# Down pass of a mixture of experts: one half of the features in 64 rows of a bank, the last pair's halves in two banks, the one-hot rows ahead of the down condition

## The chip, the cores and the metric

The kernel runs on one core of one Trainium2 chip. The metric is the device time of one execution in microseconds (us). Three executions of the kernel before took 1164.79, 1169.04 and 1176.58 us; the median is 1169.04 us. TensorE is the matrix engine, VectorE (DVE), ScalarE (ACT) and GpSimd (POOL) do the work on vectors, SyncE (SP) issues DMAs. PSUM is the accumulator memory that TensorE writes, 8 banks of 128 rows x 512 numbers.

## The reference

Two decoder layers over 256 tokens of 1024 features. Each has a token-mixing sublayer (retention, pooling and a gated delta rule, not touched here) and a mixture of experts; each ends in a layer norm of a weighted input plus the sublayer's output. The part that matters is the mixture: a coarse top-1 over 4 groups, then a top-2 over the 4 experts of that group.

```python
combine = jnp.einsum('nk,nke->ne', weights, jax.nn.one_hot(expert_id, N_EXPERTS, dtype=f32))
out = jnp.zeros((B * T, D), f32)
for e in range(N_EXPERTS):
    hdn = jax.nn.silu(xt @ w_gate[e]) * (xt @ w_up[e])
    out = out + combine[:, e:e + 1] * (hdn @ w_down[e])
...
x = layer_norm(DEEPNORM_ALPHA * x + ffn_out, ln2_g[l], ln2_b[l], dtype)
```

## The kernel before

**Slots.** The 16 experts are worked off in 8 pairs, and two pairs make a quad q (pairs 2q and 2q+1; `second` is true for the latter). Each expert of a quad has 32 slots for tokens. A one-hot matrix (`quad_slots`, L875, made by GpSimd from quad 1 on) gathers the tokens of a quad into 128 columns (`gather`, L888).

**One pair.** `gate_up` (L1026) computes gate and up projections of both experts, four column tiles of TensorE at a time (32 columns each), into a bank `gus`; ScalarE and VectorE make silu(gate) x up (L1029, L1030). `turned` (L1035, L1037) transposes the result into `hT`. `down` (L1044) multiplies by the down weights: 4 contraction steps k, four column tiles j, 16 matmuls into `bank_t`. In before, tile j holds expert `j // 2` of the pair and half `j % 2` of the 1024 features, so a half of the features lies in two pieces of 32 rows. `store` (L1052) copies the four pieces to the rows of `y` that belong to the pair.

**One quad.** When both pairs of a quad are stored, the 128 rows of `y` are the quad's outputs by slot. `slot_rows` (L1057 to L1062) transposes the one-hot matrix into `gT2` and finds each slot's weight `wqs`, through the bank `bank_c`; `weighed` (L979, L980) scales `y` by it and splits it into a rounded part `hi` and a rest `lo`; `scatter` (L1074) adds it to the tokens' rows in the accumulators `acc` with eight matmuls. `gather` also goes through `bank_c`.

**Order.** The program is written in Python and scheduled; `tc.issue_after(x)` holds what follows back until x is issued, and instructions on one engine run in the order that results. `tc.If` is a branch on a register, taken by TensorE, VectorE and ScalarE apart, and loaded from a table of kinds for each pair (`load`, L1083). Experts with more than 32 tokens take the branch `overflow` (L990), which does a whole expert for up to 128 tokens and adds it to `acc` (L1019). The two branches of a pair stand between `gate_up` and `turned`. Weights come through a ring of 1 MB pieces (`fetch`), issued by SyncE when TensorE has freed a piece.

**The end of a layer.** After the last pair's `down` the first half of the quad (`front`, rows 0 to 63, pair 6) is scattered by eight matmuls (L1155), GpSimd zeroes those rows of `gT2` (L1156), and the last pair's output is weighed straight from `bank_t` in four pieces of 32 rows (L1160, on ScalarE L979 and on VectorE L980) and scattered (L1164). The layer norm follows: `bn_stats` (L246) over four halves, and the rest of its chain.

Of the kernel before, what the change touches and what calls it, by code (L numbers as in the profile page):

```python
# [15 lines left out]
ALU = mybir.AluOpType  # L16
AX = mybir.AxisListType
# [12 lines left out]
NE = 16  # L30
# [69 lines left out]
def trunk(ctx: ExitStack, tc: tile.TileContext, x, w_in, pool_w, pool_scale, conv_w, A_log, dt_bias, gdn_norm_w,  # L100
          w_branch, w_out, ln1_g, ln1_b, rc_w, rc_b, rf_w, rf_b, w_gate, w_up, w_down, ln2_g, ln2_b, consts, out,
          dbg=None):
    nc = tc.nc
# [202 lines left out]
    tbs = [slice(0, P), slice(P, T)]  # L306

    for l in range(DEPTH):
# [4 lines left out]
        done = None  # L313
        for b in range(2):
            done = transpose_rows(xt[:, b, :], b, split_evac(xh, xl), done)
# [54 lines left out]
        for i in range(2):  # L370
            for xp, src in enumerate((xh, xl)):
                for j in range(4):
                    k = 4 * i + j
# [371 lines left out]
        done = None  # L745
# [232 lines left out]
        def weigh(h, r, src, w):  # L978
            nc.scalar.activation(h, src, AF.Identity, scale=w)  # L979
            nc.vector.scalar_tensor_tensor(r, src, w, h, op0=ALU.mult, op1=ALU.subtract)  # L980
# [56 lines left out]
            nc.vector.tensor_copy(hT, p)  # L1037
            return hT, done

        def down(pair, hT):  # L1040
            for k in range(4):
                for j in range(4):
                    e = 2 * pair + j // 2
                    done = nc.tensor.matmul(bank_t[32 * j:32 * j + 32, :], hT[:, k, 32 * (j // 2):32 * (j // 2) + 32],  # L1044
                                            units[e][4 + k // 2][k % 2][:, sides[j % 2]], start=k == 0, stop=k == 3,
                                            tile_position=(0, 32 * j))
            return done

        def store(pair):
            for j in range(4):  # L1050
                at = 64 * (pair % 2) + 32 * (j // 2)
                nc.scalar.copy(y[at:at + 32, sides[j % 2]], bank_t[32 * j:32 * j + 32, :])  # L1052

        def slot_rows(G, q):
            p = bank_c
            for b in range(2):
                nc.tensor.transpose(p[:, tbs[b]], G[b], ident)  # L1057
            for b in range(2):
                nc.tensor.matmul(p[:, T:T + 4], G[b], comb[:, b, 4 * q:4 * q + 4], start=b == 0, stop=b == 1)  # L1059
            nc.scalar.copy(gT2[:, q % 2], p[:, 0:T])  # L1060
            nc.vector.tensor_tensor(w4, p[:, T:T + 4], C("quad"), op=ALU.mult)  # L1061
            nc.vector.tensor_reduce(wqs[q % 2], w4, axis=AX.X, op=ALU.add)  # L1062

        def weighed(q):
            for half in range(2):
                s = slice(half * 512, half * 512 + 512)
                weigh(hi[:, s], lo[:, s], y[:, s], wqs[q % 2])

        def scatter(q):
            for half in range(2):  # L1070
                s = slice(half * 512, half * 512 + 512)
                for yy in (hi, lo):
                    for b in range(2):
                        nc.tensor.matmul(acc[b][half], gT2[:, q % 2, tbs[b]], yy[:, s], start=False, stop=False)  # L1074

        wqs, w4 = (small("mx", [P, 1]), small("pg", [P, 1])), small("ce", [P, 4])
        fetch(held)
# [31 lines left out]
        for pair in range(NE // 2):  # L1109
            q, second = divmod(pair, 2)  # L1110
            own, other = gus[pair % 2], gus[(pair + 1) % 2]
            last_pair = pair == NE // 2 - 1
            some = (kinds[0] | kinds[1]) & 1
            with tc.If(some > 0):
                gate_up(pair)
            if q < 3:
                for i in range(2):
                    done = gather(xgs[(q + 1) % 2], Gs[q + 1], [4 * second + 2 * i, 4 * second + 2 * i + 1], i,
                                  bank_c[:, 256 * i:256 * i + 256])
            for i in range(2):  # L1120
                e = 2 * pair + i
                with tc.If(kinds[i] > 1):
                    overflow(e, units[e], own, other)
                if e + 1 < NE:
                    picked = picks(nc.gpsimd, e + 1)
            fetch(12 * pair + 8 + held)
            if q and not second:
                weighed(q - 1)
            with tc.issue_after(done.ins):
                hT, done = turned(pair)  # L1130
            with tc.issue_after(done.ins):
                if second:
                    slot_rows(Gs[q], q)
                elif q:
                    scatter(q - 1)
            if last_pair:
                break
            with tc.If(some > 0):
                down(pair, hT)
                store(pair)  # L1140
            fetch(12 * pair + 12 + held)
            with tc.issue_after(done.ins):
                kinds = load(plan[0:1, 2 * pair + 2:2 * pair + 4])
            if second and q < 2:
                with tc.issue_after(picked.ins):
                    Gs[q + 2] = quad_slots(q + 2)
        front, last = slice(0, 64), slice(64, 128)
        downed = down(NE // 2 - 1, hT)
        for s in sides:
            weigh(hi[front, s], lo[front, s], y[front, s], wqs[1][front])  # L1150
        with tc.issue_after(downed.ins):
# [3 lines left out]
                        nc.tensor.matmul(acc[b][half], gT2[front, 1, tbs[b]], yy[front, s], start=False, stop=False)  # L1155
        nc.gpsimd.memset(gT2[front, 1].bitcast(F32), 0.0)  # L1156
        for half, s in enumerate(sides):
            for i in range(2):
                r, at = slice(64 + 32 * i, 96 + 32 * i), 64 * i + 32 * half
                weigh(hi[r, s], lo[r, s], bank_t[at:at + 32, :], wqs[1][r])  # L1160
        for b in range(2):
            for half, s in enumerate(sides):
                for yy in (hi, lo):
# [41 lines left out]
```

## Time and profile before

| | |
|---|---|
| median of three runs | 1169.04 us |
| profiled execution, its own time | 1180.57 us |
| its span, first to last instruction | 1178.8 us |
| mean granted TensorE clock | 0.944 of full speed |
| expert stage of layer 0, of layer 1 | about 324 to 590 us, about 910 to 1170 us |

Times in a timeline are microseconds from the start of the span. A row gives start, duration, engine, line and operation; the bracket is the idle time of that engine ahead of the row and what ended it. PE is TensorE, PEld its weight loads, a `q` behind a name the engine's sequencer, which loads registers and branches. The granted clock of 1.00 is 2.4 GHz, 0.50 is 1.2 GHz.

### The profile page before, as it was taken

How to read it: one execution, taken by the hardware profiler on the slowest of the kernel's cores; microseconds unless marked ns; L12 is line 12 of the kernel's file. 1: busy time of each engine (PE TensorE's matmuls, PEld its weight loads, DVE VectorE, ACT ScalarE, POOL GpSimd, SP SyncE). 2: the span in 40 equal slices, each digit the busy share in tenths (PEclk: the TensorE clock that was granted, in tenths of full speed). 3: DMA queues.
4: the chain of work that ended last, by engine and by line, in shares of the span. 5: the costliest groups of instructions: out<-in, count | busy, mean ns of one | idle time of the engine just before them, and what ended most of it. 6: DMA issues, size and time to landing. Idle time of an engine off the chain costs nothing. (4 is left out here: it accounts for less than half of the span.)

```text
span 1178.8 us, 15440 instructions
## 1 busy us (share of the span) xinstructions
PE 1061.1 (90%) x5595; PEld 705.6 (60%) x5595; DVE 470.0 (40%) x962; ACT 394.9 (33%) x618; POOL 174.8 (15%) x226
## 2 busy tenths in 40 slices
PE   7999989999789798899979999999997789799995
PEld 6778678877444354544457777788774444354442
DVE  5786356557401110111267773565565001001014
ACT  4774354453210211111147552544542111202111
POOL 2030030210401101000010400202103110100011
PEclk9999989999889898999979999999999979899996
DMA  9634457657478998849265253675665693947931
GB/s 328 210 117 142 161 196 250 196 197 259 175 273 315 393 391 304 326 144 391 82 233 178 83 179 108 232 253 193 215 221 209 240 394 128 394 153 267 357 108 37
DMA packets 112789, 266.20 MB, mean 226 GB/s; under 512 B 4760, under 2 KB 5184, under 8 KB 112672
## 3 DMA queue, kind: packets, MB, share of 16 engines
q1 hardware_dynamic: 111136, 261.14, 62.0%
q0 software_dynamic: 1248, 3.01, 1.0%
q8 instruction: 69, 1.13, 0.4%
q10 hardware_dynamic: 288, 0.52, 0.1%
q14 instruction: 48, 0.39, 0.1%
HBM read 290.88 MB, written 1.05 MB: 248 GB/s over the span
## 5 line engine op out<-in xcount | busy, mean ns | idle before, releaser
L292 DVE TENSOR_TENSOR W<-R,W 128x1024 fp32r<-128x1024 f32 x148 | 184.2, 1247 | 111.7 <-PE a L298 88.0
L291 ACT CAST W<-R 128x1024 fp32r<-128x1024 f32 x150 | 157.5, 1053 | 168.5 <-PE a L297 148.8
L296 PE MATMUL a<-W,X 128*128 128x512 f32 x504 | 202.4, 403 | 3.0 <-ACT W L291 2.8
L297 PE MATMUL a<-W,X 128*128 128x512 f32 x504 | 200.4, 399 | 0.0
L298 PE MATMUL a<-W,X 128*128 128x512 f32 x496 | 194.1, 398 | 4.1 <-DVE W L292 4.0
L984 POOL TENSOR_SCALAR s_wsm<-cst,s_pos 128x128 f32<-128x128 f32 x64 | 45.9, 727 | 450.0 <-PE t L1003 243.5
L296 PEld LDWEIGHTS a<-W,X 128*128 128x128 f32 x504 | 95.9, 190 | 25.9 <-ACT W L291 4.3
L298 PEld LDWEIGHTS a<-W,X 128*128 128x128 f32 x496 | 93.7, 189 | 26.7 <-DVE W L292 7.8
L297 PEld LDWEIGHTS a<-W,X 128*128 128x128 f32 x504 | 95.6, 190 | 20.8 <-issue 2.3
L1052 ACT COPY yh<-t 32x512 f32<-32x512 f32 x56 | 32.3, 577 | 113.7 <-PE t L1044 113.2
L888 PE MATMUL t<-t,xt 128*128 128x128 f32 x240 | 40.0, 323 | 19.1 <-DVE s_ce L1061 12.8
L888 PEld LDWEIGHTS t<-t,xt 128*128 128x128 f32 x240 | 35.5, 227 | 29.1 <-issue 19.8
L1026 PE MATMUL g<-M,X 128*32 128x512 f32 x256 | 42.4, 686 | 9.3 <-DVEq L1099 9.3
L1044 PE MATMUL t<-M,zs 128*32 128x512 f32 x256 | 49.1, 757 | 1.3 <-DVE zs L1037 1.3
L1026 PE MATMUL t<-M,X 128*32 128x512 f32 x288 | 42.7, 593 | 0.0
L998 DVE TENSOR_TENSOR ul<-ul,t 128x256 f32<-128x256 f32 x14 | 5.3, 417 | 91.8 <-PE t L995 91.8
L1044 PE MATMUL t<-R,zs 128*32 128x512 f32 x160 | 39.5, 800 | 0.7 <-issue 0.7
L1030 DVE TENSOR_TENSOR ul<-ul,t 64x512 f32<-64x512 f32 x8 | 5.5, 692 | 83.1 <-ACT ul L1029 55.9
L1026 PE MATMUL g<-R,X 128*32 128x512 f32 x160 | 37.8, 626 | 0.0
L298 PE MATMUL a<-W,yh 128*128 128x512 f32 x96 | 37.4, 389 | 0.0
L296 PE MATMUL a<-W,yh 128*128 128x512 f32 x96 | 37.3, 389 | 0.0
L297 PE MATMUL a<-W,yl 128*128 128x512 f32 x96 | 37.3, 389 | 0.0
(534 smaller groups left out, 1688.7 us busy)
## 6 DMA issues: line engine op xcount, KB each, us to landing
R<-in_w_in_dram SPq DMA_DIRECT2D x55, 1024.0 KB
M<-in_w_gate_dram SPq DMA_DIRECT2D x34, 1024.0 KB
M<-in_w_up_dram SPq DMA_DIRECT2D x34, 1024.0 KB
M<-in_w_down_dram SPq DMA_DIRECT2D x32, 1024.0 KB
R<-in_w_down_dram SPq DMA_DIRECT2D x20, 1024.0 KB
R<-in_w_gate_dram SPq DMA_DIRECT2D x18, 1024.0 KB
R<-in_w_branch_dram SPq DMA_DIRECT2D x12, 1024.0 KB
R<-in_w_up_dram SPq DMA_DIRECT2D x12, 1024.0 KB
```

The lines of the kernel that those rows point to most:

```text
L291: nc.scalar.copy(h, src)
L292: nc.vector.tensor_sub(lo, src, h)
L296: nc.tensor.matmul(acc, hi, wh, start=first, stop=False)
L297: nc.tensor.matmul(acc, lo, wh, start=False, stop=False)
L298: nc.tensor.matmul(acc, hi, wl, start=False, stop=last)
L888: done = nc.tensor.matmul(view[:, i, :], xks[b][:, k, :], picks[b], start=b == 0, stop=b == 1)
L984: last = eng.tensor_scalar(gg[:, b, :], iota, start, pos[:, b, e:e + 1], op0=ALU.add, op1=ALU.is_equal)
L998: nc.vector.tensor_mul(hoT[:, s], hoT[:, s], bank_c[:, s])
L1026: nc.tensor.matmul(p[32 * j:32 * j + 32, :], xgs[e // 4 % 2][:, k, e % 4 * SLOTS:(e % 4 + 1) * SLOTS], units[e][j // 2 + 2 * (k // 4)][k % ...
L1030: nc.vector.tensor_mul(hh[64:128, :], hh[64:128, :], p[64:128, :])
L1044: done = nc.tensor.matmul(bank_t[32 * j:32 * j + 32, :], hT[:, k, 32 * (j // 2):32 * (j // 2) + 32], units[e][4 + k // 2][k % 2][:, sides[ ...
L1052: nc.scalar.copy(y[at:at + 32, sides[j % 2]], bank_t[32 * j:32 * j + 32, :])
```

## The change

Four edits. (1) `down` gives tile j half `j // 2` and expert `j % 2`, so that one half of the features fills 64 neighbouring rows, and `store` is two copies of 64 x 512 in place of four of 32 x 512. (2) For the last pair the two halves go to two banks, `bank_t` and `bank_c`, and it is weighed in two pieces of 64 rows in place of four. (3) The condition around `down` is held back until `ready`, the last instruction of `slot_rows` or `scatter` of that pair. (4) In the last quad `weighed(2)`, `scatter(2)` and `slot_rows(3)` are written ahead of the overflow branches of pairs 6 and 7.

```diff
-        def down(pair, hT):
+        def down(pair, hT, banks):
             for k in range(4):
                 for j in range(4):
-                    e = 2 * pair + j // 2
-                    done = nc.tensor.matmul(bank_t[32 * j:32 * j + 32, :], hT[:, k, 32 * (j // 2):32 * (j // 2) + 32],
-                                            units[e][4 + k // 2][k % 2][:, sides[j % 2]], start=k == 0, stop=k == 3,
+                    e = 2 * pair + j % 2
+                    done = nc.tensor.matmul(banks[j // 2][32 * j:32 * j + 32, :], hT[:, k, 32 * (j % 2):32 * (j % 2) + 32],
+                                            units[e][4 + k // 2][k % 2][:, sides[j // 2]], start=k == 0, stop=k == 3,
                                             tile_position=(0, 32 * j))
         def store(pair):
-            for j in range(4):
-                at = 64 * (pair % 2) + 32 * (j // 2)
-                nc.scalar.copy(y[at:at + 32, sides[j % 2]], bank_t[32 * j:32 * j + 32, :])
+            r = slice(64 * (pair % 2), 64 * (pair % 2) + 64)
+            for half, s in enumerate(sides):
+                nc.scalar.copy(y[r, s], bank_t[64 * half:64 * half + 64, :])
...
+            def quarter():
+                if second:
+                    return slot_rows(Gs[q], q)
+                if q:
+                    return scatter(q - 1)
+                return done
+
+            if q == 3:
+                if not second:
+                    weighed(q - 1)
+                ready = quarter()
             for i in range(2):
                 e = 2 * pair + i
                 with tc.If(kinds[i] > 1):
...
-            if q and not second:
+            if 0 < q < 3 and not second:
                 weighed(q - 1)
             with tc.issue_after(done.ins):
                 hT, done = turned(pair)
-            with tc.issue_after(done.ins):
-                if second:
-                    slot_rows(Gs[q], q)
-                elif q:
-                    scatter(q - 1)
+            if q < 3:
+                with tc.issue_after(done.ins):
+                    ready = quarter()
             if last_pair:
                 break
-            with tc.If(some > 0):
-                down(pair, hT)
+            with tc.issue_after(ready.ins), tc.If(some > 0):
+                down(pair, hT, [bank_t] * 2)
                 store(pair)
...
-        downed = down(NE // 2 - 1, hT)
+        ends = (bank_t, bank_c)
+        downed = down(NE // 2 - 1, hT, ends)
...
         for half, s in enumerate(sides):
-            for i in range(2):
-                r, at = slice(64 + 32 * i, 96 + 32 * i), 64 * i + 32 * half
-                weigh(hi[r, s], lo[r, s], bank_t[at:at + 32, :], wqs[1][r])
+            weigh(hi[last, s], lo[last, s], ends[half][64 * half:64 * half + 64, :], wqs[1][last])
```

How the program's order moves, at the three places of which the prediction speaks. In the rows, `t`, `g` and `a` are banks of PSUM, `mix` and `yl` are `hi` and `lo`, `yh` is `y`, `zs` is `hT`, `t_240` is `gT2`, `M` and `R` are weights. A bracket names what the instruction waits for.

TensorE, pair 1 of layer 0, from `slot_rows` to the first matmul of `down`, before:

```order
L1057 MATMUL t_2297<-cst,t_239_2229 128x128 x2
L1059 MATMUL t_2297<-s_comb_2282,t_239_2229 128x4 x2
L1138 REGISTER_ALU x2
L1138 COMPARE_AND_BRANCH
L1044 MATMUL t_2296<-M_6_82,zs_2299 32x512 [waits DMAHW1_49,DMAHW4_49,DVE_49,Activation_49]
```

The same place in the change:

```order
L1057 MATMUL t_2297<-cst,t_239_2229 128x128 x2
L1059 MATMUL t_2297<-s_comb_2282,t_239_2229 128x4 x2
L888 MATMUL t_2297<-t_239_2229,xt 128x128 [waits DVE_49,Pool_49]
L1148 REGISTER_ALU x2
L1148 COMPARE_AND_BRANCH
L1044 MATMUL t_2296<-M_6_82,zs_2299 32x512 [waits DMAHW4_49,DMAHW1_49]
```

One of the eight matmuls that gather for the next quad (L888), which waits for VectorE and GpSimd, has come to stand between `slot_rows` and the condition; the other seven stay behind `down`. Pair 3 and both pairs of layer 1 read the same.

ScalarE, the same pair, before:

```order
L1138 REGISTER_ALU x2
L1138 COMPARE_AND_BRANCH
L1052 COPY yh_2291<-t_2296 32x512 [waits DVE_49,PE_49,Pool_49]
L1052 COPY yh_2291<-t_2296 32x512 x3
L1138 UNCONDITIONAL_BRANCH
L1138 UNCONDITIONAL_BRANCH [waits Activation_49]
L1060 CAST t_240_2230<-t_2297 128x256 [waits DVE_49,PE_49]
L892 COPY X_219_2149<-t_2297 128x256 [waits DVE_49,PE_49]
```

In the change:

```order
L1060 CAST t_240_2230<-t_2297 128x256 [waits DVE_49,PE_49]
L1148 REGISTER_ALU x2
L1148 COMPARE_AND_BRANCH
L1052 COPY yh_2291<-t_2296 64x512 [waits PE_49,Pool_49]
L1052 COPY yh_2291<-t_2296 64x512
L1148 UNCONDITIONAL_BRANCH
L1148 UNCONDITIONAL_BRANCH [waits Activation_49]
L892 COPY X_219_2149<-t_2297 128x256 [waits DVE_49,PE_49]
```

The cast that frees `bank_c` (L1060) has moved from behind the condition and its four copies to ahead of it, and the copies are two; VectorE's two small instructions on `bank_c` (L1061, L1062) have moved in the same way.

TensorE, end of pair 5 into `gate_up` of pair 6, layer 0, before:

```order
L1138 UNCONDITIONAL_BRANCH
L1138 UNCONDITIONAL_BRANCH [waits PE_49]
L1083 TENSOR_LOAD s_rmv_2247
L1114 REGISTER_ALU x2
L1114 COMPARE_AND_BRANCH
L1026 MATMUL g_2298<-R_1_72,X_219_2149 32x512 [waits DMAHW2_49,DMAHW0_49,Activation_49]
```

In the change:

```order
L1148 UNCONDITIONAL_BRANCH [waits PE_49]
L1074 MATMUL a_2131<-mix_273_2327,t_240_2230 128x512 [waits Activation_49]
L1074 MATMUL a_2133<-mix_273_2327,t_240_2230 128x512
L1074 MATMUL a_2132<-mix_273_2327,t_240_2230 128x512 [waits Activation_49]
L1074 MATMUL a_2131<-yl_2328,t_240_2230 128x512 [waits DVE_49]
L1074 MATMUL a_2133<-yl_2328,t_240_2230 128x512
L1074 MATMUL a_2134<-mix_273_2327,t_240_2230 128x512
L1074 MATMUL a_2132<-yl_2328,t_240_2230 128x512 [waits DVE_49]
L1074 MATMUL a_2134<-yl_2328,t_240_2230 128x512
L1084 TENSOR_LOAD s_rmv_2247
L1115 REGISTER_ALU x2
L1115 COMPARE_AND_BRANCH
```

All eight matmuls of `scatter(2)` now stand between `down` of pair 5 and the load of pair 6's kinds; before, three stood ahead of `down` of pair 6 and five behind it. `weighed(2)` has moved with them, behind the store of pair 5 on ScalarE. In pair 6, `slot_rows(3)` now stands behind `down`, where before it stood between `turned` and `down` of pair 7.

## Rows read from the trace of the kernel before

**Rows 1.** The page, busy time and share of the span of each engine.

```profile
PE 1061.1 (90%) x5595; PEld 705.6 (60%) x5595; DVE 470.0 (40%) x962; ACT 394.9 (33%) x618; POOL 174.8 (15%) x226
```

**Rows 2.** Waits of TensorE, expert stages of layers 0, 1 (total, times, longest).

```profile
PE t L888 <- DVE s_ce L1061: 6.3, 2, 3.2
...
PE t L888 <- DVE s_ce L1061: 6.5, 2, 3.2
```

**Rows 3.** Timeline, layer 0, pair 1 into pair 2 (start, us, engine, line, idle).

```profile
380.84 0.51 PE L1059 MATMUL t<-s_comb,t 128*128 128x4 f32 x4
...
381.27 3.74 PE L1044 MATMUL t<-M,zs 128*32 128x512 f32 x32
381.56 2.70 POOL L875 TENSOR_SCALAR t<-cst,s_rst 128x32 f32<-128x32 f32 x8
...
385.09 2.34 ACT L1052 COPY yh<-t 32x512 f32<-32x512 f32 x4 [6.77 <-PE t L1044]
...
388.17 1.83 PE L888 MATMUL t<-t,xt 128*128 128x128 f32 x8 [3.16 <-DVE s_ce L1061]
390.04 0.37 ACT L892 COPY X<-t 128x256 f32<-128x256 f32 x1 [2.21 <-PE t L888]
...
390.46 1.79 PE L888 MATMUL t<-t,xt 128*128 128x128 f32 x8 [0.46 <-ACT X L892]
```

**Rows 4.** Stretches, layer 0: us, busy by engine, granted clock, DMA share, GB/s.

```profile
534.40:536.40 2.00, 0.07 (x2) 0.07 (x2) 0.69 (x1) 0.65 (x2) 1.70 (x3) 1.00 1.04 391
...
538.60:543.90 5.30, 5.30 (x33) 1.88 (x32) 0.18 (x1) 0.00 (x0) 0.00 (x0) 0.68 1.04 384
...
463.30:466.70 3.40, 3.40 (x20) 0.78 (x22) 0.42 (x1) 0.00 (x0) 0.00 (x0) 0.50 1.05 388
```

**Rows 5.** Timeline, layer 0, pair 5 into pair 7.

```profile
527.28 0.59 PE L1026 MATMUL g<-R,X 128*32 128x512 f32 x1
...
527.65 2.34 ACT L1052 COPY yh<-t 32x512 f32<-32x512 f32 x4 [6.76 <-PE t L1044]
...
536.34 1.34 ACT L979 ACTIVATE mix<-yh,s_mx 128x512 fp32r<-128x512 f32 x2 [1.22 <-DVEq L1122]
...
536.91 0.42 DVE L1037 COPY zs<-g 128x256 f32<-128x256 f32 x1 [1.07 <-PE g L1035]
...
537.37 1.42 DVE L980 SCALAR_TENSOR_TENSOR yl<-yh,s_mx,mix 128x512 fp32r<-128x512 f32 x2
...
538.62 5.35 PE L1044 MATMUL t<-M,zs 128*32 128x512 f32 x32
...
545.26 4.05 PE L1026 MATMUL t<-M,X 128*32 128x512 f32 x33
```

**Rows 6.** Timeline, layer 0, the last pair's tail.

```profile
586.11 0.49 PE L1155 MATMUL a<-mix,t 64*128 64x512 f32 x1
586.22 0.68 ACT L979 ACTIVATE mix<-t,s_pg 32x512 fp32r<-32x512 f32 x1 [1.47 <-PE t L1044]
...
587.70 0.68 ACT L979 ACTIVATE mix<-t,s_pg 32x512 fp32r<-32x512 f32 x1 [0.81 <-DVE yl L980]
...
588.70 0.73 PE L1164 MATMUL a<-mix,t 128*128 128x512 f32 x2 [0.48 <-POOL t L1156]
...
589.76 1.29 DVE L246 BATCH_NORM_STATS2 s_lnst<-a 128x6 f32<-128x512 f32 x2 [0.59 <-PE a L1164]
590.01 1.04 ACT L291 CAST W<-R 128x1024 fp32r<-128x1024 f32 x1 [1.63 <-DMA R<-in_w_in_dram]
...
594.99 1.30 DVE L246 BATCH_NORM_STATS2 s_lnst<-a 128x6 f32<-128x512 f32 x2 [0.95 <-PE a L1164]
```

**Rows 7.** One line, L1083: register loads on TensorE's sequencer (ns min/median/max).

```profile
L1083 PEldq TENSOR_LOAD <-s_rmv x16: 538/545/557, 317.9 to 1139.9; - x16
```

**Rows 8.** Timeline, layer 1, the last pair's tail.

```profile
1163.26 0.73 PE L1164 MATMUL a<-mix,t 128*128 128x512 f32 x2 [0.48 <-POOL t L1156]
...
1168.28 1.29 DVE L246 BATCH_NORM_STATS2 s_lnst<-a 128x6 f32<-128x512 f32 x2 [0.93 <-PE a L1164]
```

More of the change, by code (lines that the diff above doesn't have):

```diff
@@ L1061, in slot_rows @@
             nc.vector.tensor_tensor(w4, p[:, T:T + 4], C("quad"), op=ALU.mult)
-            nc.vector.tensor_reduce(wqs[q % 2], w4, axis=AX.X, op=ALU.add)
+            return nc.vector.tensor_reduce(wqs[q % 2], w4, axis=AX.X, op=ALU.add)
         def weighed(q):
@@ L1073, in scatter @@
                     for b in range(2):
-                        nc.tensor.matmul(acc[b][half], gT2[:, q % 2, tbs[b]], yy[:, s], start=False, stop=False)
+                        done = nc.tensor.matmul(acc[b][half], gT2[:, q % 2, tbs[b]], yy[:, s], start=False, stop=False)
+            return done
         wqs, w4 = (small("mx", [P, 1]), small("pg", [P, 1])), small("ce", [P, 4])
@@ L1119, in trunk @@
                                   bank_c[:, 256 * i:256 * i + 256])
+            def quarter():
[3 more added lines that the diff above has]
+                    return scatter(q - 1)
+                return done
+            if q == 3:
+                if not second:
+                    weighed(q - 1)
+                ready = quarter()
             for i in range(2):
```

## The prediction

> **What bounds the kernel now.** I read the page first: TensorE is busy 90% of the span [rows 1], so time is won where it stands still or runs at half clock. Next the waits of TensorE in the two expert stages: no transfer of any size is on the list, and beside the branches the largest wait that the change touches is the gather L888 waiting for the small VectorE instruction L1061, twice in each layer, 3.2 us each time [rows 2]. The timelines show the three places where the change acts. I call them A, B and C.
>
> A is the way from pair 1 to pair 2 and from pair 3 to pair 4: four places. `down` ends at 381.27 + 3.74 = 385.01; TensorE then stands for 3.16 us, because ScalarE makes four copies (2.34 us) before the cast L1060 and VectorE's L1061, which free the bank that the gather needs. A second wait of 0.46 us follows, for ScalarE's copy L892 [rows 3]. After such waits the clock is down: once the stretch behind it ran at 0.50 for 3.4 us [rows 4].
>
> B is the way from pair 5 over pair 6 to pair 7, once in a layer. There `gate_up` of pair 6 begins at 527.28, before ScalarE even starts to copy the result of `down` at 527.65: no gap at all [rows 5].
>
> C is the tail of a layer. The last pair's four weighings take turns on ScalarE and VectorE, since all read one bank: ScalarE's second piece starts only at 587.70, released by VectorE, though its first ended at 586.90. In layer 0 the third piece stands moreover behind a cast of the next layer's weights, which waits for a transfer until 590.01 [rows 6].
>
> The sum is made against the profiled execution, 1180.57 us; it is 11.5 us slower than the median of the three runs (1169.04), so I carry the difference over to the median.
>
> **A: the gather's wait, four places.** Cast and VectorE's pair now run as soon as `slot_rows` ends (380.84 + 0.51 = 381.35), so the 3.16 us behind `down` go. In exchange one gather matmul stands ahead of `down`, with `down` queued behind it. It needs four of GpSimd's eight one-hot instructions L875, which begin at 381.56 and take 2.70 us: half is 1.35, so 382.91. I allow 0.3 for the matmul and the branch behind it: `down` starts at 383.2 in place of 381.27 and ends at 383.2 + 3.74 = 386.9. Then seven gather matmuls; the fifth still waits for L892, now behind two copies in place of four. Rows do not make a ScalarE instruction longer: 128 rows take 1.34 / 2 = 0.67 us [rows 5], 32 rows 0.68 [rows 6]. So two copies take half of 2.34, 1.17, plus 0.37: 386.9 + 0.1 + 1.17 + 0.37 = 388.5. The last gathers take 1.79: 390.3, in place of 390.46 + 1.79 = 392.25 [rows 3]. That is 1.95 per place, say 2.0. No row has a wait ahead of `down`, so bounds: if it drops the clock there, `down` loses 3.4 us of time at half speed, 1.7, and 0.3 is left; if no clock is lost, the 1.7 of the stretch at 0.50 come on top, 3.7 [rows 4]. I take 2.0, the middle, because waits of this length are seen with the fall and without. Sum of A: -8.0 (-1.2 to -14.8).
>
> **B: scatter(2) moves ahead of pair 6, twice.** Added: TensorE waits for the chain behind `down` of pair 5. From 527.65 two copies, 1.17; ScalarE's first L979, 0.67, to 529.5, its second to 530.2; VectorE's two L980, 1.42 / 2 = 0.71 each, end at 530.9 [rows 5]. The last two matmuls wait for that, and behind them TensorE's sequencer has yet to load pair 6's kinds, 0.55 [rows 7], and to branch: 531.7. Queued behind it is `gate_up` of pair 6, which everything of that pair waits for. Price: 531.7 - 527.3 = 4.4. Removed: `down` of pair 6 need not wait for the scatter. `hT` is ready at 536.91 + 0.42 = 537.33, `down` began at 538.62: 1.2 saved after 0.1 for the signal. Behind it the five matmuls went until 545.26, after `down` ended at 538.62 + 5.35 = 543.97: 1.3 [rows 5]. In their stead come four small ones of `slot_rows(3)`, about 0.9 with the turn of bank, by 0.51 for the second half of them [rows 3]: 0.4 saved. In pair 7 they hid behind VectorE's copy of `hT`; I count nothing for their going. B is 4.4 - 1.2 - 0.4 = 2.8 per layer.
>
> Then the clock: the stretch from 534.40 stood nearly idle for 2 us, and of the 5.3 us from 538.60 the mean clock is 0.68 [rows 4]. 0.32 of 5.3 is 1.7 us lost. B's new wait is like it, so I add 1.7 with a chance of 0.7, 1.2. Sum of B: +8.0 for two layers (+5.6 to +9.0).
>
> The Trainium skill (TensorEngine Tiling (Array Packing), Key Properties) says that a change of tiling mode drains TensorE. `scatter(2)` between `down` and `gate_up` makes two such changes where there was none; the trace agrees in so far as `gate_up` began within the last wave of `down`. By the rule four changes would cost some 0.3 us each, an estimate from that overlap, and the sum would end at 1163; by the rows they lie inside gaps already counted, and it ends at 1162.
>
> **C: the tail, twice.** The work up to L1155 stays. The two halves lie in two banks, so ScalarE does them back to back: 586.22 + 0.68 + 0.68 = 587.6; VectorE, 0.71 each, ends at 588.4. L1164 starts at 588.70 as before, held by GpSimd's memset, and now all eight matmuls follow at once. The four `bn_stats` run from about 589.6 for 1.29 + 1.30, to 592.2; before, the last two ended at 594.99 + 1.30 = 596.29 [rows 6]. Layer 0: -4.1. The next layer's first weights were there at 590.01, ahead of its new beginning. Layer 1: from 1163.26 the first `bn_stats` comes about 0.9 later, 1164.2, and the four end at 1166.8, in place of 1168.28 + 1.29 = 1169.57 [rows 8]: -2.8. Sum of C: -6.9 (-2.8, if layer 0 hides it, to -7.5).
>
> **Costed at nothing.** In pairs 2 and 4 the five scatter matmuls move from behind `down` to ahead of it; the same matmuls stand on the path, and the shorter store makes up for the later `down`. Bounds: with all four copies kept there, ScalarE would be 1.17 late [rows 5], and a gain is left out because no wait goes. The new order of column tiles changes no count: `gate_up` already alternates the two experts from tile to tile, 33 records in 4.05 us [rows 5], `down` has 32 in 3.74 [rows 3]; the difference, 0.2 per pair either way, is the bound, and I take 0 because both include other work's gaps. SyncE issues the same transfers in the same order.
>
> **The sum.** -8.0 + 8.0 - 6.9 = -6.9: 1173.7 for the profiled execution, 1162 at the median, -0.6%.
>
> **The rivals.** (1) A gives nothing: the hoisted gather's wait drops the clock in `down`. For it: the wait stands behind small transposes. Against: it is half as long as the one it replaces. -1.2 + 8.0 - 6.9 = -0.1, so 1169. (2) A gives everything and B keeps its clock: -14.8 + 5.6 - 6.9 = -16.1, so 1153. For it: TensorE has eight matmuls inside B's wait; against: they are spread over 4 us. (3) Slower: B's wait drops the clock for all of `gate_up` of pair 6, from 527.28 to 534.40 [rows 4, 5], 7.1 us more. B is then 2 x (2.8 + 7.1) = 19.8, the total +4.9: 1174. It decides once B is over 14.9, a loss of clock of 4.7 us in each layer. Against: no stretch of rows 4 lost more than 1.7. The Trainium skill (TensorE: Matmul & The Clock Gate, Part 1: The HAM clock gate) makes low clock the resting state, released by activity alone; by that, a wait with few matmuls in it costs the work behind it, as in (3), and rows 4 agree. (4) Layer 0's tail hides its gain behind the next layer's weights: -2.8, 1166. Against: [rows 6], 590.01.
>
> **How the numbers follow.** Forecast 0.45 (1158 to 1166), (1) 0.20, (2) 0.22, (3) 0.08, (4) 0.05. 1% of 1169 is about 12 us, about what a measurement of this kernel can tell from no change. Faster by more than that needs a time under 1157: most of (2), 0.20. Slower by it needs over 1181, beyond (3): 0.05. Within: 0.75. The range leaves out the far end of (2) and (3): 1152 to 1171.
>
> **What would show it.** A: the wait of L888 for L1061 is gone; a new one of 1 to 2 us ahead of `down` in pairs 1 and 3, released by GpSimd. B: L1074 waits for ScalarE and VectorE behind pair 5, and `gate_up` of pair 6 begins 4 to 5 us after `down`. C: two L979 and two L980 on the last bank rows, overlapping, and `bn_stats` in one run. I am wrong if the gather ahead of `down` waits for all eight of GpSimd's instructions, if B's gap is over 6 us, or if layer 1's first matmul does not come earlier against the end of pair 7.

## The result: 1161.4 us, 1.0% faster

| | before | the change |
|---|---|---|
| median of 16 runs each | 1175.08 us | 1161.37 us |
| lowest and highest | 1164.79, 1179.44 us | 1156.88, 1167.58 us |
| ratio, 95% interval | | 0.990 (0.987 to 0.993) |
| profiled execution, its own time | 1180.57 us | 1162.66 us |
| its span, mean granted clock | 1178.8 us, 0.944 | 1160.9 us, 0.962 |

The ratio stands for 11.7 us less (8.7 to 14.8). With more runs the median of the kernel before rose by 6 us, from the 1169.04 that the prediction started from. So the gain was 5 us larger than the 6.9 of the sum, and that the time itself lies beside the predicted 1162 is luck: the two differences cancel.

The page of the change, busy time and share of the span of each engine; [rows 1] are those of before:

```profile
PE 1045.4 (90%) x5595; PEld 703.6 (61%) x5595; DVE 466.9 (40%) x958; ACT 376.1 (32%) x586; POOL 174.9 (15%) x226
```

ScalarE has 32 instructions less, 28 copies and 4 weighings. TensorE has as many as before and is busy 15.7 us less; its mean granted clock is 0.962 in place of 0.944.

Waits of TensorE in the expert stage of layer 0, after (waiting line, releaser, total us, times, longest), then of layer 1:

```profile
PE t L888 <- POOL t L875: 3.3, 2, 1.6
PE a L1074 <- ACT mix L979: 2.7, 3, 2.1
...
PE a L1074 <- ACT mix L979: 2.9, 3, 2.1
PE t L888 <- POOL t L875: 2.2, 2, 1.1
```

The wait of the gather for L1061 [rows 2] is gone. In its place the gather ahead of `down` waits for GpSimd, twice in a layer, and the scatter behind pair 5 waits 2.1 us for ScalarE, once in a layer.

A in the timeline of the change, layer 0, pair 1 into pair 2; the rows of before are [rows 3]:

```profile
382.32 0.51 PE L1059 MATMUL t<-s_comb,t 128*128 128x4 f32 x4
382.87 0.37 ACT L1060 CAST t<-t 128x256 fp32r<-128x256 f32 x1 [3.06 <-PE t L1059]
383.05 2.70 POOL L875 TENSOR_SCALAR t<-cst,s_rst 128x32 f32<-128x32 f32 x8
...
384.48 0.49 PE L888 MATMUL t<-t,xt 128*128 128x128 f32 x2 [1.65 <-POOL t L875]
384.92 3.76 PE L1044 MATMUL t<-M,zs 128*32 128x512 f32 x32
...
388.61 0.94 PE L888 MATMUL t<-t,xt 128*128 128x128 f32 x6
...
388.81 1.17 ACT L1052 COPY yh<-t 64x512 f32<-64x512 f32 x2 [5.57 <-PE t L1044]
390.00 0.37 ACT L892 COPY X<-t 128x256 f32<-128x256 f32 x1
390.43 1.16 PE L888 MATMUL t<-t,xt 128*128 128x128 f32 x8 [0.88 <-ACT X L892]
```

The cast runs at 382.87, right behind `slot_rows`. `down` starts 384.92 - (382.32 + 0.51) = 2.09 us after `slot_rows` ends, and TensorE goes on into the gather without a gap. The copy L892 comes behind two copies, which take 1.17 us.

B in the timeline of the change, layer 0, end of pair 5 into pair 6; before, `gate_up` began at 527.28, ahead of ScalarE's copy at 527.65 [rows 5]:

```profile
523.06 1.18 ACT L1052 COPY yh<-t 64x512 f32<-64x512 f32 x2 [3.40 <-PE t L1044]
...
524.27 1.34 ACT L979 ACTIVATE mix<-yh,s_mx 128x512 fp32r<-128x512 f32 x2
525.02 1.41 DVE L980 SCALAR_TENSOR_TENSOR yl<-yh,s_mx,mix 128x512 fp32r<-128x512 f32 x2 [4.97 <-ACT mix L979]
525.04 1.12 PE L1074 MATMUL a<-mix,t 128*128 128x512 f32 x3 [2.11 <-ACT mix L979]
...
526.87 1.05 PE L1074 MATMUL a<-yl,t 128*128 128x512 f32 x2
527.85 1.06 PE L1026 MATMUL g<-R,X 128*32 128x512 f32 x1
```

`gate_up` now begins at 527.85, 4.8 us behind the start of the copies at 523.06; before it was 0.4 us ahead of that start. The new price is 5.2 us.

C in the timeline of the change, layer 0, the last weighings and the four `bn_stats`, then the same of layer 1; the rows of before are [rows 6, 8]:

```profile
587.00 0.49 PE L1166 MATMUL a<-mix,t 64*128 64x512 f32 x1
587.07 1.39 ACT L979 ACTIVATE mix<-t,s_pg 64x512 fp32r<-64x512 f32 x2 [3.60 <-PE t L1044]
587.78 1.53 DVE L980 SCALAR_TENSOR_TENSOR yl<-t,s_pg,mix 64x512 fp32r<-64x512 f32 x2 [3.26 <-ACT mix L979]
589.60 0.51 PE L1173 MATMUL a<-mix,t 128*128 128x512 f32 x1 [0.48 <-POOL t L1167]
590.37 1.89 DVE L246 BATCH_NORM_STATS2 s_lnst<-a 128x6 f32<-128x512 f32 x3 [1.05 <-PE a L1173]
592.42 0.64 DVE L246 BATCH_NORM_STATS2 s_lnst<-a 128x6 f32<-128x512 f32 x1
...
1149.04 1.89 DVE L246 BATCH_NORM_STATS2 s_lnst<-a 128x6 f32<-128x512 f32 x3 [1.04 <-PE a L1173]
1151.09 0.64 DVE L246 BATCH_NORM_STATS2 s_lnst<-a 128x6 f32<-128x512 f32 x1
```

From the first matmul of the first scatter (L1155 before, L1166 after) to the end of the last `bn_stats` it is 593.06 - 587.00 = 6.06 us, where it was 596.29 - 586.11 = 10.18 [rows 6].

### A ledger by place

For this table I took from the trace of each kernel the starts of the same instructions and subtracted the durations between them in before: A from the first L1035 of pair 1 to that of pair 2 and from pair 3 to pair 4 (so that a low clock in the `gate_up` behind counts too), "2, 4" the same for pairs 2 and 4, B from pair 5 to pair 7, C from the first matmul of the first scatter to the end of the last `bn_stats`; both layers together, in us. Each row is one profiled execution. That of before was 5.5 us above its median, and places in which a kernel has the code of before still differ by up to 3.3, so a single entry is good to about 3 us; the ratios are better. The kernels are those of the next section.

| kernel | A | 2, 4 | B | C | ratio (95%) |
|---|---|---|---|---|---|
| the change | -14.1 | -4.7 | +9.8 | -7.0 | 0.990 (0.987 to 0.993) |
| change_again | -10.0 | -3.9 | +7.9 | -7.0 | 0.989 (0.984 to 0.994) |
| layout_alone (edit 1, tail in two pieces out of one bank) | -9.4 | -3.8 | -0.3 | -6.8 | 0.984 (0.979 to 0.989) |
| old_turns | -12.8 | -4.4 | +0.3 | -6.7 | 0.981 (0.978 to 0.985) |
| four_copies | -0.2 | +2.1 | +2.4 | -6.8 | 0.993 (0.991 to 0.996) |
| tail_alone | +0.2 | +2.1 | +1.5 | -6.9 | 0.998 (0.994 to 1.002) |
| edit3_alone | -5.7 | -0.7 | -0.8 | -0.2 | 1.001 (0.998 to 1.004) |
| edit4_alone | -3.3 | -3.2 | +14.2 | -0.4 | 1.014 (1.009 to 1.019) |
| edits_1_3 | -8.3 | -3.6 | -0.6 | -6.8 | 0.978 (0.975 to 0.981) |

### The profile page after: what moved, and what is told of

It reads as the page before. It is cut to its first block, busy times and chain, and to the rows that moved or that the text cites. A ratio compares the mean times of both kernels' runs of the same rounds, so it can differ in the third digit from the quotient of the medians.

```text
span 1160.9 us, 15400 instructions
## 1 busy us (share of the span) xinstructions
PE 1045.4 (90%) x5595; PEld 703.6 (61%) x5595; DVE 466.9 (40%) x958; ACT 376.1 (32%) x586; POOL 174.9 (15%) x226
## 3 DMA queue, kind: packets, MB, share of 16 engines
HBM read 290.88 MB, written 1.05 MB: 251 GB/s over the span
## 5 line engine op out<-in xcount | busy, mean ns | idle before, releaser
L1044 PE MATMUL t<-M,zs 128*32 128x512 f32 x256 | 49.1, 714 | 3.0 <-DVE zs L1037 2.6
L888 PE MATMUL t<-t,xt 128*128 128x128 f32 x240 | 36.3, 296 | 13.7 <-ACT X L892 7.3
L1052 ACT COPY yh<-t 64x512 f32<-64x512 f32 x28 | 16.2, 580 | 96.2 <-PE t L1044 95.9
L888 PEld LDWEIGHTS t<-t,xt 128*128 128x128 f32 x240 | 30.6, 200 | 26.4 <-issue 10.1
L1044 PE MATMUL t<-R,zs 128*32 128x512 f32 x160 | 37.7, 709 | 1.3 <-ACT mix L979 1.3
L890 DVE COPY X<-t 128x256 f32<-128x256 f32 x16 | 6.8, 425 | 79.4 <-PE t L888 75.2
```

The lines of the kernel that those rows point to most:

```text
L888: done = nc.tensor.matmul(view[:, i, :], xks[b][:, k, :], picks[b], start=b == 0, stop=b == 1)
L890: nc.vector.tensor_copy(dst[:, at:at + len(ks), :], view)
L1044: done = nc.tensor.matmul(banks[j // 2][32 * j:32 * j + 32, :], hT[:, k, 32 * (j % 2):32 * (j % 2) + 32], units[e][4 + k // 2][k % 2][:, s ...
L1052: nc.scalar.copy(y[r, s], bank_t[64 * half:64 * half + 64, :])
```

## The experiments

My theory was that of the prediction: edit 1 and edit 3 share A, edit 4 costs B, and the tail gives C whatever else is done. The rivals were that the tail's gain is lost again, that B would cost the same wherever scatter(2) stands, and that one edit carries all.

### tail_alone: only the last pair

```diff
-        downed = down(NE // 2 - 1, hT)
+        ends = (bank_t, bank_c)
+        downed = down(NE // 2 - 1, hT, ends)
...
-            for i in range(2):
-                r, at = slice(64 + 32 * i, 96 + 32 * i), 64 * i + 32 * half
-                weigh(hi[r, s], lo[r, s], bank_t[at:at + 32, :], wqs[1][r])
+            weigh(hi[last, s], lo[last, s], ends[half][64 * half:64 * half + 64, :], wqs[1][last])
```

> The kernel before with nothing but the new tail: for the last pair alone, one half of the features in 64 rows, the two halves in two banks, two weighings on each engine in place of four. Own theory (the tail is worth what the rows of the last pair say, and is independent of the rest): -4.1 us in layer 0 and -2.8 us in layer 1, together -6.9, so about 0.994 of the kernel before. Rival (the next layer's weights or the clock behind the tail take layer 0's part back): -2.8, 0.9975.

The trace has the -4.1 and -2.8 to the hundredth (C is -6.9). The ratio is 0.998 (0.994 to 1.002), so of the expected 0.994 the interval holds only the edge. A part of it is in the trace: with `slot_rows(3)` still ahead of the last `down`, the half of it that goes to `bank_c` waits until that bank is read. This is TensorE's weight load in the last `down` of layer 0 (L1045 and L1069 are L1044 and L1061 there):

```profile
582.91 0.57 PEld L1045 LDWEIGHTS t<-R,zs 128*32 128x32 f32 x10 [0.51 <-DVE s_ce L1069]
```

From L1035 of the last pair to the first scatter it takes 0.62 us more than before in layer 0. So without edit 4 the second bank costs about what this row shows; with four_copies, below, the tail alone gives 0.993.

### layout_alone: edit 1, the tail in two pieces out of one bank

```diff
-                    e = 2 * pair + j // 2
+                    e = 2 * pair + j % 2
...
-            for j in range(4):
-                at = 64 * (pair % 2) + 32 * (j // 2)
-                nc.scalar.copy(y[at:at + 32, sides[j % 2]], bank_t[32 * j:32 * j + 32, :])
+            r = slice(64 * (pair % 2), 64 * (pair % 2) + 64)
+            for half, s in enumerate(sides):
+                nc.scalar.copy(y[r, s], bank_t[64 * half:64 * half + 64, :])
...
+            weigh(hi[last, s], lo[last, s], bank_t[64 * half:64 * half + 64, :], wqs[1][last])
```

> The kernel before with 64-row halves and nothing else: two stores in place of four, the last pair weighed in two pieces of 64 rows, but out of one bank; order of all else as before. Own theory: the wait of the gather behind `down` in pairs 1 and 3 is shorter by two copies, 1.17 us at four places, -4.7; and at the tail the number of pieces decides, not the banks: four turns of about 0.7 us on one bank end at about 586.2 + 2.9 = 589.1, when the second scatter begins anyway, so -6.9 as with two banks. Together -11.6, 0.990: as much as the whole change. Rival (two banks are what frees the tail): the tail keeps half its loss, -4.7 - 3.4 = -8.1, 0.993.

0.984: edit 1 and the two pieces at the tail are together worth 18.5 us (12.6 to 24.2 of 1171), more than the whole change by the middle values; the interval of old_turns, below, up to 0.985, ends ahead of that of the change, from 0.987. The banks do next to nothing: C is -6.8 out of one bank and -7.0 out of two. The four weighings of layer 0 take turns, and the scatter starts as if they did not:

```profile
578.40 0.68 ACT L979 ACTIVATE mix<-t,s_pg 64x512 fp32r<-64x512 f32 x1 [1.52 <-PE t L1044]
579.12 0.75 DVE L980 SCALAR_TENSOR_TENSOR yl<-t,s_pg,mix 64x512 fp32r<-64x512 f32 x1 [1.40 <-ACT mix L979]
579.90 0.68 ACT L979 ACTIVATE mix<-t,s_pg 64x512 fp32r<-64x512 f32 x1 [0.82 <-DVE yl L980]
580.51 0.30 POOL L1156 MEMSET t<- 64x256 f32 x1 [5.48 <-PE a L1155]
580.61 0.76 DVE L980 SCALAR_TENSOR_TENSOR yl<-t,s_pg,mix 64x512 fp32r<-64x512 f32 x1 [0.75 <-ACT mix L979]
580.86 0.50 PE L1162 MATMUL a<-mix,t 128*128 128x512 f32 x1 [0.48 <-POOL t L1156]
```

The last weighing ends at 581.37 and is hidden behind GpSimd's memset and the first matmuls. What counted was that there are two pieces on each engine instead of four.

### scatter_back: weighed(2) and scatter(2) in pair 6 again

```diff
-            if q == 3:
-                if not second:
-                    weighed(q - 1)
-                ready = quarter()
+            if last_pair:
+                ready = quarter()
...
-            if 0 < q < 3 and not second:
+            if q and not second:
                 weighed(q - 1)
...
-            if q < 3:
+            if not last_pair:
```

> The change with weighed(2) and scatter(2) back in pair 6, between `turned` and `down`, as in pairs 2 and 4; slot_rows(3) stays ahead of pair 7. Own theory: the wait of 2.1 us behind `down` of pair 5 and the scatter behind it cost 8.4 us for two layers (profiled offsets: +5.5 and +2.9), so this is faster than the change by 6 to 9 us: about 0.983 of the kernel before. Rival (scatter(2) costs the same in pair 6, since its eight matmuls stand on the path in either place): 0.988 to 0.990, as the change.

0.985 (0.979 to 0.990), B +0.6 in place of +9.8 and +7.9. It is the price of the wait and not of the eight matmuls, which this kernel has too. The ratio alone would not settle it, since its interval touches that of the change; the trace and edit4_alone do.

### onehot_vector: what the gather ahead of `down` waits for

```diff
-            if q == 0:
+            if q != 1:
                 for b in range(2):
-                    nc.vector.tensor_tensor(G[:, b], own_pos[:, b, 0:4, None].to_broadcast([P, 4, SLOTS]),
+                    nc.vector.tensor_tensor(G[:, b], own_pos[:, b, 4 * q:4 * q + 4, None].to_broadcast([P, 4, SLOTS]),
```

> The change with the one-hot matrices of quads 2 and 3 made by VectorE (two instructions of 128 x 128) in place of GpSimd (eight of 128 x 32). Own theory: the gather matmul that now stands ahead of `down` in pairs 1 and 3 waits 1.65 us (layer 0) and 1.10 us (layer 1) for GpSimd; VectorE is done about 1.1 us sooner, so -4 us in all: 0.986 of the kernel before. Rival (the matmul is held by the bank that ScalarE and VectorE must free first): the wait stays above 1 us, 0.990.

TensorE's wait in pair 1 of layer 0:

```profile
PE t L888 <- DVE s_ce L1061: 0.7, 1, 0.7
```

It fell from 1.65 to 0.7 us, so GpSimd was the releaser and the bank comes next. The ratio 0.9885 (0.984 to 0.993) cannot be told from that of the change: the expected -4 is within the interval, and so is nothing.

### four_copies and old_turns: which part of edit 1

four_copies against layout_alone:

```diff
-            r = slice(64 * (pair % 2), 64 * (pair % 2) + 64)
-            for half, s in enumerate(sides):
-                nc.scalar.copy(y[r, s], bank_t[64 * half:64 * half + 64, :])
+            for j in range(4):
+                at = 64 * (pair % 2) + 32 * (j % 2)
+                nc.scalar.copy(y[at:at + 32, sides[j // 2]], bank_t[32 * j:32 * j + 32, :])
```

> layout_alone with four copies of 32 x 512 in place of two of 64 x 512; `down` in the new order of tiles, the last pair weighed in two pieces. Theory 1 (the copies carry the gain of layout_alone, the tail the rest): the wait behind `down` in pairs 1 and 3 is 3.2 us again, only the tail's -7 is left, 0.994. Theory 2 (the new order of tiles keeps the clock up in `down`, as the traces of layout_alone and of the change show in pairs 2 and 4 of layer 1): another -3 to -6 from that, 0.989 to 0.991.

old_turns against layout_alone:

```diff
-                for j in range(4):
+                for j in (0, 2, 1, 3):
                     e = 2 * pair + j % 2
```

> layout_alone with the matmuls of `down` issued in the turns 0, 2, 1, 3 of tiles, so that two neighbours in time belong to one expert as in the kernel before; tiles and copies as in layout_alone. Theory 1 (the turns of experts do not matter): 0.984 as layout_alone, and `down` of pairs 2 and 4 of layer 1 takes 3.7 to 4.2 us. Theory 2 (alternating the experts keeps the clock up): `down` there takes 5.4 us again as before, in all 3 to 6 us slower than layout_alone, 0.987 to 0.989.

Theory 1 in both. With four copies only the tail is left, 0.993 (-7.9 us, 4.5 to 11.2; C shows -6.8). With two copies and the old turns of experts all is there, 0.981. Both ran on one chip against the same runs of before: the two copies are worth 0.993 - 0.981 = 0.012, 14 us. The two kernels differ in the turns of the tiles too, which by old_turns do not matter; the fastest run of four_copies, 1164.7 us, is slower than the slowest of old_turns, 1157.23.

### edits_1_3 and edits_1_3_onehot: without edit 4

```diff
-            if q == 3:
-                if not second:
-                    weighed(q - 1)
-                ready = quarter()
...
-            if 0 < q < 3 and not second:
+            if q and not second:
                 weighed(q - 1)
...
-            if q < 3:
-                with tc.issue_after(done.ins):
-                    ready = quarter()
+            with tc.issue_after(done.ins):
+                ready = quarter()
...
-        ends = (bank_t, bank_c)
+        ends = (bank_t, bank_t)
```

> The change without edit 4 and with the tail out of one bank: 64-row halves, two stores, the condition around `down` held back until `ready`. Against layout_alone (0.984) it differs by edit 3 alone. Own theory: the remaining 2.0 us wait behind `down` in pairs 1 and 3 is exchanged for 1.1 to 1.65 us ahead of it, and the clock no longer falls there: 4 to 7 us more than layout_alone, 0.979 of the kernel before. Rival (the new wait ahead of `down` takes it back): 0.984, as layout_alone.

0.978 (0.975 to 0.981), a median of 1149.8 us beside 1177.3 of before: 26 us less by the ratio, where the change has 12. That is better than the kernel before and the change. Against old_turns, which has edit 1 and the two-piece tail and ran on the same chip, the ratio is 0.004 lower, 4 us, and the intervals overlap; in the traces A is not shorter for it (-8.3 against -12.8). Beside edit 1, edit 3 is worth little.

> The same with the one-hot matrices of quads 2 and 3 made by VectorE, which shortened the wait ahead of `down` to 0.7 us in onehot_vector. Own theory: a further 1 to 2 us (onehot_vector was 0.9885 against 0.990 of the change): 0.978. Rival: no difference to edits_1_3.

0.980 (0.977 to 0.983): no difference to edits_1_3.

### edit4_alone, edit3_alone, change_again, edits_1_3_odd: one chip

edit4_alone and edit3_alone are the lines of these edits in the diff of the change, put into the kernel before; change_again has no edit.

> The change itself once more, unaltered, for a comparison on one chip with the three below. All theories: 0.990 of the kernel before (0.987 to 0.993), and in its trace a wait of 2.1 us behind `down` of the sixth pair of each layer.

0.989 (0.984 to 0.994): the same as the first time.

> The kernel before with edit 4 alone: weighed(2), scatter(2) and slot_rows(3) ahead of the overflow branches of pairs 6 and 7; old tiles, four copies, old tail. Own theory (the edit is a loss by itself): the new wait behind `down` of pair 5 is longer than in the change by two copies, 2.1 + 1.2 = 3.3 us, so 8.4 to 12 us slower in all: 1.007 to 1.010. Rival (it costs only beside the other edits, because they made it the last wait): 1.000 to 1.002.

1.014 (1.009 to 1.019): 16 us slower, more than expected. The wait behind pair 5, layer 0, then the rows of that stretch:

```profile
PE a L1074 <- ACT mix L979: 4.3, 2, 4.1
...
529.21 2.35 ACT L1052 COPY yh<-t 32x512 f32<-32x512 f32 x4 [6.83 <-PE t L1044]
532.43 1.34 ACT L979 ACTIVATE mix<-yh,s_mx 128x512 fp32r<-128x512 f32 x2 [0.48 <-DVE s_mx L1062]
533.21 1.43 PE L1074 MATMUL a<-mix,t 128*128 128x512 f32 x3 [4.08 <-ACT mix L979]
```

The wait is 4.1 us and not the 3.3 of my expectation: behind the four copies stand here also the cast and VectorE's L1062 of `slot_rows`, which edit 3 puts ahead of the condition. So beside edits 1 and 3 edit 4 is cheaper, by the ledger 8 to 10 us in place of 14.

> The kernel before with edit 3 alone: the condition around `down` held back until `ready`; old tiles, four copies, old tail. Own theory: the wait of 3.2 us behind `down` goes, one of 1.1 to 1.65 us ahead of it comes, but behind `down` the copy L892 now ends behind four copies, and the second half of the gather waits about 2 us for it: some 0.8 us per place, -3 us, 0.997; more (to 0.992) if the clock stays up. Rival (edit 3 carries what the change gains in pairs 1 to 4, 14 + 5 us): 0.984.

1.001 (0.998 to 1.004): nothing. The rows of A, layer 0, pair 1:

```profile
384.90 0.49 PE L888 MATMUL t<-t,xt 128*128 128x128 f32 x2 [1.64 <-POOL t L875]
...
385.34 5.45 PE L1044 MATMUL t<-M,zs 128*32 128x512 f32 x32
...
390.88 2.34 ACT L1052 COPY yh<-t 32x512 f32<-32x512 f32 x4 [7.21 <-PE t L1044]
393.24 0.37 ACT L892 COPY X<-t 128x256 f32<-128x256 f32 x1
...
393.67 1.16 PE L888 MATMUL t<-t,xt 128*128 128x128 f32 x8 [2.01 <-ACT X L892]
```

The 3.2 us wait is replaced by 1.64 ahead of `down` and 2.01 behind it, for the copy L892 that stands behind four copies. And `down` takes 5.45 us, not 3.74: the clock fell in it. In layer 1 A is 6.3 us shorter in this trace; the twelve runs show nothing of it, the ratio decides, and why the two differ is open.

> edits_1_3 with the condition held back in pairs 1 and 3 alone (and 5); in pairs 2 and 4 three matmuls of the scatter stand ahead of `down` and five behind it, as before. Theory 1 (what the change gains in pairs 2 and 4, 4.7 us in its trace, comes from the order of the scatter): 4 us slower than edits_1_3, 0.982. Theory 2 (it is the clock in `down`, which stays up once the store is two copies, whatever the order): 0.978 to 0.979, as edits_1_3.

0.983 (0.978 to 0.987). By its middle value the ratio is nearer the first theory, and its interval holds both; the trace speaks for the second. Pairs 2 and 4 gain 3.6 us with the old order of the scatter, as much as edits_1_3 with the new one.

## Why the prediction was right, step by step

**C is exact in the traces.** -4.1 and -2.8 were predicted, -4.12 and -2.85 are in the trace of the change; the ratio of tail_alone shows less of it, that of four_copies all. C lies between -6.7 and -7.0 in all kernels of the ledger that have two pieces. The next layer's weights did not take it back. One reason given was wrong: the banks. The working had ScalarE run both pieces back to back because they lie in two banks; layout_alone takes turns on one bank and gains the same.

**B is right in sum, within some 2 us.** +8.0 predicted (+5.6 to +9.0); +9.8, above that range, and +7.9 in two traces. The wait came where it was forecast. `gate_up` came 5.2 us later and not 4.4, mainly because the last two scatter matmuls, which the working gave no time, ran 1.05 us. That was at the lower clock. In change_again, the same program, they ran 0.62 us at the higher one, and TensorE then stood for 0.36 us:

```profile
530.20 0.62 PE L1074 MATMUL a<-yl,t 128*128 128x512 f32 x2
531.19 0.59 PE L1026 MATMUL g<-R,X 128*32 128x512 f32 x1 [0.36 <-issue]
```

The load of the kinds, which the working gave 0.55, runs beside these matmuls in that trace (529.99 to 530.53), and the branch behind it ends at 531.02, in the gap; in the change the slow matmuls hide both. Of the 1.6 us that pair 6 was to save in each layer, the two traces show 1.6 and 1.7 in layer 1, but 0.6 and 1.4 in layer 0, where `down` of pair 6 ran 6.54 and 5.75 us in place of 5.35. The clock behind the wait, in `gate_up` of pair 6 of the change, layers 0 and 1 (columns as in [rows 4]):

```profile
527.90:535.90 8.00, 8.00 (x65) 1.99 (x64) 0.00 (x0) 0.00 (x0) 0.00 (x0) 0.88 1.05 391
1087.40:1095.60 8.20, 8.20 (x66) 2.18 (x65) 0.00 (x0) 0.00 (x0) 0.00 (x0) 0.86 1.03 394
```

0.12 x 8.0 = 1.0 and 0.14 x 8.2 = 1.1 us lost, where 1.2 was allowed; in layer 0 of change_again this `gate_up` kept 1.00. Rival (3) wanted 7.1.

By the rule of the Trainium skill that the prediction weighed (TensorEngine Tiling (Array Packing), Key Properties), a change of mode drains the array. In the rows of B of the change `gate_up` starts at 527.85 and the last scatter matmul ends, as modelled, at 526.87 + 1.05 = 527.92: no gap of 0.3 us is to be seen. The 0.36 us of change_again may hold a drain beside the branch; no run separates them.

**A is under-sized, and credited to the wrong edit.** -8.0 predicted (-1.2 to -14.8); -14.1 and -10.0 in the two traces of the change. The steps themselves hold: GpSimd's wait was put at 1.55 and is 1.65. `down` was to start 1.93 us later than before; it started 0.08 us ahead of the end of `slot_rows` [rows 3] and now starts 2.09 behind it, 2.2 later. The second half of the gather waits behind two copies. But the text told A as the work of edit 3, with the two copies as a detail of it. By the ratios edit 3 alone gives nothing, and the two copies give 14 us, of which the sum had 4 x 1.17 = 4.7.

What the sum mis-sized is the clock, and the place is layer 1: there A is -9.2 in the change and -9.6 in change_again, where -4.0 was forecast for a layer and 2 x 3.7 = 7.4 was its far bound. In the kernel before, the clock fell behind `down` in all four places, while the prediction took the price from one stretch of 3.4 us, which began only with `gate_up` [rows 4]. The gather and `gate_up` behind `down` of pairs 1 and 3 of layer 1, before, then in the change:

```profile
955.60:968.00 12.40, 11.90 (x81) 5.55 (x81) 0.51 (x2) 0.37 (x1) 0.00 (x0) 0.75 1.03 398
1031.00:1043.30 12.30, 11.81 (x81) 5.61 (x81) 0.50 (x2) 0.37 (x1) 0.00 (x0) 0.76 0.89 331
...
948.10:958.10 10.00, 9.08 (x79) 4.41 (x79) 0.42 (x1) 1.53 (x3) 0.00 (x0) 1.00 1.01 386
1016.90:1027.10 10.20, 9.27 (x79) 7.18 (x79) 0.43 (x1) 1.53 (x3) 0.00 (x0) 1.00 1.03 396
```

0.25 x 12.4 = 3.1 and 0.24 x 12.3 = 3.0 us, an estimate from these rows, were lost there before, and nothing is now. Nor did the new wait ahead of `down` cost clock in layer 1: the granted clock was at 0.50 in `slot_rows` already, before as in the change, and over `down` it was 0.56 and 0.59 before, 0.66 and 0.74 in the change.

In layer 0 the new wait can cost what it saves. In A the prediction kept to the middle between "drops the clock in `down`" and "no clock lost", and both happen. `down` of pairs 1 and 3 of layer 0 in the change, then in change_again, the same program:

```profile
384.90:388.70 3.80, 3.80 (x34) 1.94 (x33) 0.00 (x0) 0.00 (x0) 0.85 (x3) 1.00 1.04 331
453.10:456.90 3.80, 3.80 (x34) 1.92 (x33) 0.00 (x0) 0.00 (x0) 0.88 (x3) 1.00 1.05 400
...
383.30:388.70 5.40, 5.40 (x34) 2.55 (x33) 0.00 (x0) 0.00 (x0) 0.80 (x3) 0.68 0.98 356
453.70:459.80 6.10, 6.10 (x34) 1.36 (x33) 0.00 (x0) 0.00 (x0) 0.52 (x2) 0.59 1.05 395
```

With the clock up A gains 2.1 and 2.7 us at these two places, with the clock down 0.4 and 0.1: the forecast's 2.0 in one execution, and the case of rival (1) in the other.

Over all fourteen traces, in the four places of A: behind a wait of 3.2 us the clock fell in gather and `gate_up` in all 16 places of the four kernels that have this wait (means 0.73 to 0.85), behind the 2.0 us of layout_alone and old_turns in 5 of 8, and in the eight traces with edit 3 in none of 32. In six of these eight the gather waits about 1.6 us for GpSimd ahead of `down` in layer 0, and there `down` was slow in 8 of 12 places. So in layer 0 edit 3 moved the loss from behind `down` into it.

**Pairs 2 and 4, costed at nothing.** The traces show -4.7 and -3.9. The order of the scatter is not the cause: edits_1_3_odd has the old order and -3.6, and edit4_alone, whose code there is that of before, has -3.2. It is the clock in `down` of layer 1, here in pair 2 of before and of edit4_alone:

```profile
999.20:1004.70 5.50, 5.50 (x34) 3.19 (x33) 0.19 (x1) 0.00 (x0) 0.00 (x0) 0.69 1.05 397
...
1004.60:1008.60 4.00, 4.00 (x34) 1.96 (x33) 0.20 (x1) 0.00 (x0) 0.00 (x0) 1.00 1.04 399
```

0.31 x 5.5 = 1.7 us where it fell. So the moved matmuls cost nothing that these traces can show, and the sum lacked a term for the clock.

**The sum.** A -10 to -14, B +8 to +10, C -7, with -4 to -5 in pairs 2 and 4, gives -13 and -16 in the two traces, against an execution of before that was 5.5 us slow; the ratio gives 11.7 us less. Predicted were 6.9 with a range of the time from 1152 to 1171. The direction and "within 1%" (0.990, at its edge) hold; the term that was mis-sized is A, by the clock. That 1161 came so near to 1162 is luck, since the start of the sum was 6 us too low.

**Open.** Why the clock falls in `down` in one execution and stays up in another of the same program, and why it does so in pairs 2 and 4 of layer 1 in the kernels above. The two copies go with a clock that stays up there in every kernel that has them; edit3_alone and edit4_alone have four, and it stays up there too. Another order, in which the gather stands behind `down` without the wait for GpSimd, was not tried on the chip.

## What to carry to other kernels

Shorten the work that stands between two users of a bank before moving instructions around it: half as many copies, each as long as before, gave 14 us, and holding a branch back for an earlier cast gave nothing by itself. A step that is moved ahead of its old place takes its own inputs along: scatter(2) had a whole pair's time to wait in, and ahead of pair 6 it put ScalarE's and VectorE's chain on TensorE's path, 8 to 16 us. When edits are made together, run each alone; here the kernel with the lowest ratio, edits_1_3, leaves out edit 4 and the second bank of edit 2.

## What the runs showed of the hardware that was not expected

A wait of 1.6 us ahead of 32 matmuls cost its own length in one execution and 1.7 to 2.4 us more in another of the same program, by the granted clock alone (1.00, or 0.68 and 0.59 over the matmuls); the levels behind these means are 2.4 and 1.2 GHz. So the price of a short wait of TensorE is best taken as two values. The clock goes with the spread between runs: of the 16 runs of the change the fastest, 1156.88 us, had a mean granted clock of 0.966, and the slowest, 1167.58 us, one of 0.958.

Two engines that share a bank lost little by it: between the turns of ScalarE and VectorE in layout_alone lie 579.12 - (578.40 + 0.68) = 0.04 us.
